# The second mixture of experts of a two-block network: rooms of 192, 96 and 32 tokens, cut into chunks of 128, 64 and 32

## The chip, the cores and the metric

The kernel runs on one core of one Trainium2 chip. The metric is the device time of one execution in microseconds; where several executions were timed, the median stands. The core has five engines with a queue of instructions each: TensorE (PE; its weight loads are listed apart, as PEld), VectorE (DVE), ScalarE (ACT), GpSimd (POOL) and SyncE (SP), which issues nearly all of the transfers from the chip's memory.

## The reference

The program is a network of two blocks on 256 tokens of width 1024. The first block has a convolution, an attention with forgetting, and a mixture of 32 experts, four for each token. The second has two layers: a hybrid mixer with a dense feed-forward part, and a hybrid mixer with a mixture of eight experts, two for each token. The change touches that last mixture alone:

```python
def moe_swiglu(x, router_w, router_b, w1, w3, w2):     # x: 256 tokens x 1024
    logits = (x @ router_w) + router_b                 # 8 experts
    top_vals, top_idx = lax.top_k(logits, 2)
    top_w = jax.nn.softmax(top_vals, axis=-1)
    gate = jnp.sum(jax.nn.one_hot(top_idx, 8) * top_w[..., None], axis=-2)
    out = jnp.zeros_like(x)
    for e in range(8):                                 # w1, w3: 1024 x 1408, w2: 1408 x 1024
        out = out + gate[..., e:e + 1] * ((silu(x @ w1[e]) * (x @ w3[e])) @ w2[e])
    return out
```

All is float32. Only the tokens that chose an expert have a gate above zero, so an expert may be computed on these tokens alone. With the inputs of the reference the eight experts are chosen by 57, 123, 49, 9, 8, 49, 165 and 52 tokens (worked out from the reference).

## The kernel before

The second mixture is the function `moe2`, the last stage of the program. Its experts are taken in eight places, p0 to p7. Place p0 is always expert 0, so that its weights can be loaded before the routing is known; the others are filled by rank, rank 1 being the expert with the most tokens. `RANK2` gives the rank that a place takes, and `ROOM2` how many tokens the place has room for:

```python
ROOM2 = [128, 256, 64, 64, 128, 128, 128, 64]
RANK2 = [0, 1, 7, 6, 2, 3, 4, 5]
```

Tokens over a place's room would go to a loop at the end (L1816 and on), whose number of turns is read at run time; one turn computes a chunk of up to 128 tokens.

The weights of an expert come in 17 loads: 11 of 1 MB, one for each slice of 128 of the hidden width 1408 (`w13`, 1024 x 256: w1 and w3 side by side), five of 1 MB with two such slices of w2 each, and one of 0.5 MB with the last. All go through SP's queue into a ring of eight tiles; a load waits until the tile that it overwrites has been read by all who read it. Each generator below yields after a load and its work, and `run` steps through it, so that two experts can be put into one order by turns.

There are three forms of an expert:

- `expert_all` (room 256, p1) takes all tokens, without gathering. `split` (L322 to L328) first makes two float32r halves of each weight tile, a cast on ACT (L325) and a difference on DVE (L328) for each 128x1024, and `mm3` (L304 to L307) multiplies by three products of the halves. 
- `expert_128` (p0, p4, p5, p6) has split weights too. Its tokens are gathered: `gather2` multiplies the transposed tokens by a matrix of zeros and ones (L1598) for a group of places at once. The tokens stand as the stationary operand and the weights stream, 256 columns at a time. `finish` applies silu and the product, and transposes the result (L1718 is the same step in the next form), and `spread` (L1650 to L1665) splits the outcome into halves `my0h` and `my0l` (for 128 also `my1h` and `my1l`), multiplies it by the matrix that puts tokens back (L1662), and adds it into `xres` with the gate.
- `expert_64` (p2, p3, p7) uses the weights unsplit as float32. Its 64 tokens take half of TensorE's columns, so two loads are worked side by side (L1732), one slice in columns 0 to 63 and one in 64 to 127; in the w2 part (L1748) the two halves of the output stand side by side.

The order of the work is written out by hand. After p0, p1 runs with p2 and p3 by turns: one load of p1, then two of p2 (later p3). Then come p4, p5, p6 and p7, one after another. Gathers stand at the half of p0 (for p2, p3, p7), of p1 (for p4, p5) and of p5 (for p6):

```python
every, few = expert(1), [expert(2), expert(3)]
while run(every, 1, lambda: gather_group((4, 5))):
    for _ in range(2):
        while few and not run(few[0], 1):
            few.pop(0)
...
run(expert(4))
run(expert(5), 99, lambda: gather_group((6,)))
run(expert(6))
run(expert(7))
```

## Time and profile before

| | us |
|---|---|
| median of 3 runs (lowest, highest) | 2324.02 (2322.54, 2326.08) |
| the profiled execution | 2327.09 |
| its span, from the first instruction to the last | 2325.3 |
| second mixture, from the first row of its gathering to the end | 1853 to 2325 |
| p0; p1 with p2 and p3; p4; p5 with a gather; p6; p7 | 58.5; 171.7; 51.5; 55.2; 50.8; 37.3 |

The stages in the last row follow one another and end at 2308.3 us; the last layer norm and the output take the rest. A profile's row of busy time says how long an engine had an instruction under way. A row of a timeline is a run of like instructions: its start, its length from the first start to the last end, engine, line, operation, the names written and read, the shape and the count. Lengths of single matmul rows overlap, since one is let in before the last has ended; what a matmul costs is read from the starts of two, or from a long run of them.

### The profile page before, as it was taken

How to read it: one execution, taken by the hardware profiler on the slowest of the kernel's cores; microseconds unless marked ns; L12 is line 12 of the kernel's file. 1: busy time of each engine (PE TensorE's matmuls, PEld its weight loads, DVE VectorE, ACT ScalarE, POOL GpSimd, SP SyncE). 2: the span in 40 equal slices, each digit the busy share in tenths (PEclk: the TensorE clock that was granted, in tenths of full speed). 3: DMA queues.
4: the chain of work that ended last, by engine and by line, in shares of the span. 5: the costliest groups of instructions: out<-in, count | busy, mean ns of one | idle time of the engine just before them, and what ended most of it. 6: DMA issues, size and time to landing. Idle time of an engine off the chain costs nothing. (4 is left out here: it accounts for less than half of the span.)

```text
span 2325.3 us, 34078 instructions
## 1 busy us (share of the span) xinstructions
PE 2158.1 (93%) x13530; PEld 1424.9 (61%) x13530; DVE 1126.3 (48%) x2048; ACT 785.4 (34%) x1313; POOL 34.9 (2%) x45
## 2 busy tenths in 40 slices
PE   6999999899999889998797999999999899999996
PEld 4888533333333333333235988998888788777983
DVE  3976222323322322322236657654665775337883
ACT  3354211101111111111104655444465564335771
POOL 0000000000000000000000010000001000000000
PEclk9999899998999989999897999999999989999998
DMA  9757689998999999999898334555533467779884
GB/s 395 282 217 271 242 321 417 416 407 344 410 416 416 416 416 412 415 415 416 367 416 335 134 109 164 182 189 183 188 130 110 166 223 275 281 298 349 330 329 197
DMA packets 122630, 697.52 MB, mean 300 GB/s; under 512 B 11120, under 2 KB 11648, under 8 KB 63936
## 3 DMA queue, kind: packets, MB, share of 16 engines
q1 hardware_dynamic: 121120, 690.54, 76.1%
q0 software_dynamic: 1344, 4.73, 0.7%
q8 instruction: 109, 1.79, 0.3%
q14 instruction: 57, 0.47, 0.1%
HBM read 694.18 MB, written 1.05 MB: 299 GB/s over the span
## 5 line engine op out<-in xcount | busy, mean ns | idle before, releaser
L328 DVE TENSOR_TENSOR wl<-w,wh 128x1024 fp32r<-128x1024 f32 (+1 forms) x393 | 476.9, 1223 | 256.7 <-ACT wh L325 247.5
L325 ACT CAST wh<-w 128x1024 fp32r<-128x1024 f32 (+1 forms) x393 | 407.4, 1044 | 304.5 <-PE acc L306 65.7
L962 PE MATMUL h<-w,xg 128*64 128x512 f32 x1280 | 302.0, 620 | 0.0
L997 PE MATMUL s<-w,hm 128*64 128x512 f32 (+1 forms) x1088 | 252.1, 651 | 17.6 <-DVE hm L985 14.1
L962 PEld LDWEIGHTS h<-w,xg 128*64 128x64 f32 x1280 | 93.7, 142 | 186.7 <-issue 182.2
L306 PE MATMUL acc<-xTl,wh 128*128 128x256 f32 x528 | 149.7, 284 | 0.0
L305 PE MATMUL acc<-xTh,wh 128*128 128x256 f32 x528 | 149.7, 283 | 0.0
L307 PE MATMUL acc<-xTh,wl 128*128 128x256 f32 x528 | 149.6, 283 | 0.0
L973 ACT COPY hs<-h 128x512 f32<-128x512 f32 x34 | 19.9, 585 | 373.2 <-PE h L962 290.5
L997 PEld LDWEIGHTS s<-w,hm 128*64 128x64 f32 (+1 forms) x1088 | 62.2, 132 | 130.8 <-issue 95.0
L956 PE MATMUL h<-w,xg 128*32 128x512 f32 x896 | 114.4, 635 | 17.6 <-DMA w<-in_wei 17.6
L973 DVE COPY hs<-h 128x512 f32<-128x512 f32 x20 | 13.8, 691 | 235.9 <-PE h L962 235.9
L910 PEld LDWEIGHTS t<-oh,xh 128*128 128x128 f32 x512 | 70.5, 209 | 76.2 <-ACT xg L911 32.2
L911 ACT ACTIVATE xg<-t,modc,a 128x128 f32<-128x128 f32 (+3 forms) x128 | 55.4, 440 | 182.2 <-PE t L910 126.4
L307 PEld LDWEIGHTS acc<-xTh,wl 128*128 128x128 f32 x528 | 99.3, 188 | 4.2 <-issue 3.1
L305 PEld LDWEIGHTS acc<-xTh,wh 128*128 128x128 f32 x528 | 99.3, 188 | 2.5 <-issue 1.5
L306 PEld LDWEIGHTS acc<-xTl,wh 128*128 128x128 f32 x528 | 99.3, 188 | 2.0 <-issue 1.1
L306 PE MATMUL f<-fxl,wh 128*128 128x256 f32 x352 | 99.9, 284 | 0.0
L305 PE MATMUL f<-fxh,wh 128*128 128x256 f32 x352 | 98.9, 282 | 0.7 <-ACT fxh L1236 0.7
L307 PE MATMUL f<-fxh,wl 128*128 128x256 f32 x352 | 99.3, 283 | 0.0
L910 PE MATMUL t<-oh,xh 128*128 128x128 f32 (+3 forms) x512 | 85.5, 309 | 14.2 <-ACT xg L911 7.1
L1011 ACT CAST ysh<-ys 128x512 fp32r<-128x512 f32 x34 | 21.0, 618 | 222.6 <-DVE ys L1010 207.4
(540 smaller groups left out, 4294.8 us busy)
## 6 DMA issues: line engine op xcount, KB each, us to landing
w<-in_wei SPq DMA_DIRECT2D x256, 1024.0 KB, 18.4
w<-in_weo SPq DMA_DIRECT2D x128, 1024.0 KB, 19.9
w<-in_wm SPq DMA_DIRECT2D x128, 1024.0 KB, 5.8
w<-in_wf SPq DMA_DIRECT2D x33, 1024.0 KB, 4.8
w<-in_w2in SPq DMA_DIRECT2D x32, 1024.0 KB, 5.1
w<-in_wada SPq DMA_DIRECT2D x24, 1024.0 KB, 9.7
w<-in_win SPq DMA_DIRECT2D x16, 1024.0 KB, 8.6
w<-in_w2out SPq DMA_DIRECT2D x8, 1024.0 KB, 4.9
```

The lines of the kernel that those rows point to most:

```text
L305: T.matmul(o, l[0], r[0], start=start, stop=False)
L306: T.matmul(o, l[0], r[1], start=False, stop=False)
L307: return T.matmul(o, l[1], r[0], start=False, stop=stop)
L325: A.copy(wh[:, :m], w[:, o:o + m])
L328: V.tensor_sub(wl[:, :m], w[:, o:o + m], wh[:, :m])
L910: T.matmul(pt[:, 0:n], xh2[:, tt, k * P:(k + 1) * P], oh[:, tt, 0:n], start=tt == 0, stop=tt == 1)
L911: taken.append(A.activation(xg[:, k, 0:n], pt[:, 0:n], AF.Identity, bias=sh2[:, k:k + 1], scale=a2[:, k:k + 1]))
L956: T.matmul(ph[0][0][32 * q:32 * q + 32, :].rearrange("p (i c) -> p i c", i=4), chunks[0][:, k], w5[:, q % 2, q // 2], start=k == 0, stop=k ...
L962: T.matmul(p[j][64 * gu:64 * gu + 64, :], xs[:, k], w[:, gu * D + j * 512:gu * D + j * 512 + 512], start=k == 0, stop=k == 7)
L973: (A.copy if j == 0 else V.tensor_copy)(hs[:, j], p[j])
L997: T.matmul(p[r, :], hm[:, kk * 2 + k], w[:, k * D + hf * 512:k * D + hf * 512 + 512], start=kk == 0 and (small or k == 0), stop=kk == 3 an ...
L1011: A.copy(yp[0], ys)
```

## The change

The rooms become 128, 192, 32, 32, 128, 64, 96 and 96 for p0 to p7, each cut into chunks of 128, 64 or 32 (`CHK2`), and the ranks are dealt anew: p2 and p3 take ranks 6 and 7, p5 rank 5, p6 and p7 ranks 3 and 4. With the counts above every expert fits its room. One generator, `expert2`, replaces the three forms: each load of weights is used for all chunks of a place. Chunks of 128 work as before with split weights; those of 64 as before with the unsplit weights of two loads; a chunk of 32 is new: it takes a quarter of TensorE's columns, so that w1 and w3 of two loads stand side by side (L1704), and in the w2 part two slices and two halves of the output (L1731). Only places with a chunk of 128 split their weights. In p1 the tiles of two loads are read twice, by the chunk of 128 as they come and by that of 64 when both are there.

p2 and p3 run by turns with p1 as before, and p5 now by turns with p4. The gathers after p0 stand at the half of p0 (p1, p2, p3), p1 (p4, p5) and p4 (p6, p7). The transposed tokens `xT` move to the buffer that the gather's operand `xtp` also uses. The loads and their order on SP's queue stay: 136 for the eight experts.

```diff
--- before.py
+++ after.py
@@ -37,8 +37,11 @@
-ROOM2 = [128, 256, 64, 64, 128, 128, 128, 64]
-RANK2 = [0, 1, 7, 6, 2, 3, 4, 5]
+CHK2 = [[(0, 128)], [(0, 128), (128, 64)], [(0, 32)], [(0, 32)], [(0, 128)], [(0, 64)], [(0, 64), (64, 32)], [(0, 64), (64, 32)]]
+ROOM2 = [sum(n for _, n in c) for c in CHK2]
+RANK2 = [0, 1, 6, 7, 2, 5, 3, 4]
...
-                xT = pair([P, 8, S], "mx", 1)
+                xT = pair([P, 8, S], "xt", 1)
...
-                        xs.append(wk.tile([P, 8, 64], F32, tag="mx64", name=nm("mx64"), bufs=3) if room == 64
-                                  else tuple(t[:, :, o:o + 128] for t in big))
+                    for _, (_, room), _ in items:
+                        xs.append(big if room == 128
+                                  else wk.tile([P, 8, room], F32, tag=f"mx{room}", name=nm(f"mx{room}"), bufs=3))
...
-                def expert_all(w13, w2, gate):
...
-                def expert_128(w13, w2, xg, item):
...
-                def expert_64(w13, w2, xg, item):
...
+                def expert2(w13, w2, xs, items):
+                    rooms = [room for _, (_, room), _ in items()]
+                    hid = [hidden_pair() if n == 128 else wk.tile([P, FT2, n], F32, tag=f"mhm{n}", name=nm("mhm"), bufs=1 if n == 64 else 2) for n in rooms]
+                    def finish(n, hp, f0, nf, ph):
+                        if n == 128:
...
+                            return
+                        r = slice(0, 64 * nf)
+                        s = wk.tile([P, P], F32, tag="mss", name=nm("mss"), bufs=3)
+                        if n == 64:
+                            A.activation(s[r], ph[r, 0:P], AF.Silu)
+                            V.tensor_tensor(s[r], s[r], ph[r, P:S], op=ALU.mult)
+                        else:
+                            A.copy(s[r], ph[r, 0:P])
                         pt = bank()
+                        T.transpose(pt[:, r], s[r], ident[r, r])
+                        if n == 64:
+                            A.copy(hp[:, f0:f0 + nf], pt[:, r].rearrange("p (f s) -> p f s", s=64))
+                        else:
+                            p4 = pt[:, r].rearrange("p (f g s) -> p f g s", g=2, s=32)
+                            s = wk.tile([P, 2, 32], F32, tag="msg", name=nm("msg"), bufs=2)
+                            A.activation(s[:, 0:nf], p4[:, :, 0], AF.Silu)
+                            V.tensor_tensor(hp[:, f0:f0 + nf], s[:, 0:nf], p4[:, :, 1], op=ALU.mult)
                     pend = []
+                    def finish_all():
+                        while pend:
+                            finish(*pend.pop(0))
                     for f0 in range(0, FT2, 2):
                         nf = min(2, FT2 - f0)
+                        phs = [bank("b", 6) for _ in rooms]
                         ws = []
                         for fi in range(nf):
                             ws.append(load(w13(f0 + fi)))
+                            if rooms[0] == 128:
+                                w = split(ws[fi], 256)
+                                for k in range(8):
+                                    mm3(phs[0][:, fi * S:(fi + 1) * S], tuple(x[:, k] for x in xs[0]), cview(w, k, 256, 0, 256), k == 0, k == 7)
                             if fi < nf - 1:
                                 yield "step"
+                        for n, x, ph in zip(rooms, xs, phs):
+                            if n == 128:
+                                continue
+                            for k in range(8):
+                                for fi, w in enumerate(ws):
+                                    if n == 64:
+                                        T.matmul(ph[64 * fi:64 * fi + 64, 0:S], x[:, k], w[:, k * S:(k + 1) * S], start=k == 0, stop=k == 7)
+                                    else:
+                                        for gu in range(2):
+                                            c = 64 * fi + 32 * gu
+                                            T.matmul(ph[c:c + 32, 0:P], x[:, k], w[:, k * S + gu * P:k * S + gu * P + P],
+                                                     start=k == 0, stop=k == 7)
+                        finish_all()
+                        pend += [(n, hp, f0, nf, ph) for n, hp, ph in zip(rooms, hid, phs)]
                         yield "step"
                     yield "half"
+                    gts = [back(item) for item in items()]
+                    pys = [[bank("b", 6) for _ in range(2 if n == 128 else 1)] for n in rooms]
                     for f0 in range(0, FT2, 2):
                         nf = min(2, FT2 - f0)
                         w = load(w2(f0, nf), nf * D)
+                        if rooms[0] == 128:
+                            wp = split(w, D, nf * D)
+                        if rooms[0] < 128:
+                            finish_all()
+                        for n, hp, py in zip(rooms, hid, pys):
+                            for fi in range(nf):
+                                f = f0 + fi
+                                for hf in range(2):
+                                    c = fi * D + hf * 512
+                                    if n == 128:
+                                        mm3(py[hf], sl(hp, slice(None), f), cview(wp, fi, D, hf * 512, hf * 512 + 512), f == 0, f == FT2 - 1)
+                                    elif n == 64:
+                                        T.matmul(py[0][64 * hf:64 * hf + 64, :], hp[:, f], w[:, c:c + 512], start=f == 0, stop=f == FT2 - 1)
+                                    else:
+                                        r = 64 * hf + 32 * fi
+                                        T.matmul(py[0][r:r + 32, :], hp[:, f], w[:, c:c + 512], start=f0 == 0, stop=f >= FT2 - 2)
+                            finish_all()
                         yield "step"
+                    for n, py, gt in zip(rooms, pys, gts):
+                        spread(py, *gt, [(0, slice(0, P)), (1, slice(0, P))] if n == 128 else [(0, slice(0, 64)), (0, slice(64, P))])
...
+                def items(p):
+                    return [(columns(route2.posm, p), c, columns(route2.gp, p)) for c in CHK2[p]]
...
-                    gather_group((2, 3, 7))
-                run(expert(0), 99, half0)
-                every, few = expert(1), [expert(2), expert(3)]
-                while run(every, 1, lambda: gather_group((4, 5))):
+                    gather_group((1, 2, 3))
...
+                most, few = expert(1), [expert(2), expert(3)]
+                while run(most, 1, lambda: gather_group((4, 5))):
                     for _ in range(2):
                         while few and not run(few[0], 1):
                             few.pop(0)
                 while few:
                     run(few.pop(0))
-                run(expert(4))
-                run(expert(5), 99, lambda: gather_group((6,)))
+                most, few = expert(4), expert(5)
+                while run(most, 1, lambda: gather_group((6, 7))):
+                    run(few, 1)
+                run(few)
                 run(expert(6))
                 run(expert(7))
```

The next rows are TensorE's order while p1 and p2 run by turns, before: p1's product of three with all tokens as the streamed operand (`mxh`, `mxl`), then two of p2's loads at 64 wide.

```order
L305 MATMUL b_15128<-mxh_14221,wh_15124 128x256
L306 MATMUL b_15128<-mxl_14222,wh_15124 128x256
L307 MATMUL b_15128<-mxh_14221,wl_15125 128x256
L1732 MATMUL b_15185<-w_15186,mx_2494_14860 64x256
L1732 MATMUL b_15185<-w_15188,mx_2494_14860 64x256
```

After, in the same place: the chunk of 128 of p1 has its second load (`wh_15216`), and then the chunk of 64 of p1 reads the two tiles that were held for it (`w_15138`, `w_15210`).

```order
L308 MATMUL b_15136<-wh_15216,mxh_14855 128x256
L309 MATMUL b_15136<-wl_15217,mxh_14855 128x256
L310 MATMUL b_15136<-wh_15216,mxl_14856 128x256
L1700 MATMUL b_15137<-w_15138,mx_2496_14863 64x256
L1700 MATMUL b_15137<-w_15210,mx_2496_14863 64x256
```

Behind these 16 products of the chunk of 64 come 32 of p2's chunk of 32 (L1704). What was one block with all tokens and one 64 wide is now one of 128, one of 64 and one of 32.

The second place is TensorE's order where an unsplit expert goes from its last slice of w1 and w3 into w2. Before, in p7 (64):

```order
L1718 MATMUL t_18516<-cz,ms_18513 128x128
L1732 MATMUL b_18519<-w_18520,mx_2496_14862 64x256 x8
L1718 MATMUL t_18533<-cz,ms_18530 128x128
L1613 MATMUL t_18536<-cz,posm_14847 128x128 x2
L1748 MATMUL b_18541<-w_18542,mhm_18389 64x512
L1718 MATMUL t_18547<-cz,ms_18544 128x64
L1748 MATMUL b_18541<-w_18542,mhm_18389 64x512 x3
L1748 MATMUL b_18541<-w_18554,mhm_18389 64x512 x4
L833 MATMUL t_18602<-cnt_14317,perm_14316 8x1
L1748 MATMUL b_18541<-w_18560,mhm_18389 64x512 x4
```

After, in p6 (64 and 32):

```order
L1700 MATMUL b_17813<-w_17815,mx_2908_17178 64x256 x8
L1704 MATMUL b_17814<-w_17815,mx_2909_17179 32x128 x16
L1667 MATMUL t_17844<-cz,mss_17841 128x128
L1667 MATMUL t_17849<-cz,mss_17847 128x128
L1727 MATMUL b_17864<-w_17866,mhm_17489 64x512
L1619 MATMUL t_17854<-cz,posm_14847 128x128 x2
L1619 MATMUL t_17859<-cz,posm_14847 128x128 x2
L1727 MATMUL b_17864<-w_17866,mhm_17489 64x512 x2
L1667 MATMUL t_17871<-cz,mss_17868 128x64
L1667 MATMUL t_17876<-cz,mss_17874 128x64
L1727 MATMUL b_17864<-w_17866,mhm_17489 64x512
L1731 MATMUL b_17865<-w_17866,mhm_17490 32x512 x4
```

The transpositions, the two broadcasts of the positions and the blocks of each load stand twice in it, once for each chunk.

The third place is the end of the last expert. Before, its one `spread` follows the last load of w2:

```order
L1748 MATMUL b_18541<-w_18578,mhm_18389 64x512 x2
L1662 MATMUL b_18586<-my0h_18582,mgt_18539 128x512
L1662 MATMUL b_18587<-my0h_18582,mgt_18539 128x512
L1662 MATMUL b_18594<-my0h_18582,mgt_18539 128x512
L1662 MATMUL b_18595<-my0h_18582,mgt_18539 128x512
L1662 MATMUL b_18586<-my0l_18583,mgt_18539 128x512
L1662 MATMUL b_18587<-my0l_18583,mgt_18539 128x512
```

After, two follow one another, the second reading the next `my0h`:

```order
L1727 MATMUL b_18359<-w_18424,mhm_17984 64x512 x2
L1731 MATMUL b_18360<-w_18424,mhm_17985 32x512 x2
L1635 MATMUL b_18434<-my0h_18430,mgt_18352 128x512
L1635 MATMUL b_18435<-my0h_18430,mgt_18352 128x512
L1635 MATMUL b_18442<-my0h_18430,mgt_18352 128x512
L1635 MATMUL b_18434<-my0l_18431,mgt_18352 128x512
L1635 MATMUL b_18435<-my0l_18431,mgt_18352 128x512
L1635 MATMUL b_18443<-my0h_18430,mgt_18352 128x512
L1635 MATMUL b_18442<-my0l_18431,mgt_18352 128x512
L1635 MATMUL b_18443<-my0l_18431,mgt_18352 128x512
L840 MATMUL t_18470<-cnt_14317,perm_14316 8x1
L1635 MATMUL b_18454<-my0h_18450,mgt_18357 128x512
```

## Rows read from the trace of the kernel before

**Rows 1.** The page: span, and busy time by engine.

```profile
span 2325.3 us, 34078 instructions
PE 2158.1 (93%) x13530; PEld 1424.9 (61%) x13530; DVE 1126.3 (48%) x2048; ACT 785.4 (34%) x1313; POOL 34.9 (2%) x45
```

**Rows 2.** Windows of the stages p1 to p7: length, busy times, clock, DMA share, GB/s.

```profile
1941.80:2113.50 171.70, 170.10 (x1168) 126.67 (x1166) 67.54 (x115) 52.68 (x108) 0.00 (x0) 1.00 0.77 298
2113.50:2165.00 51.50, 51.28 (x357) 47.01 (x356) 47.27 (x52) 38.58 (x47) 0.00 (x0) 1.00 0.93 350
2165.00:2220.20 55.20, 54.98 (x386) 50.17 (x385) 49.32 (x62) 40.37 (x55) 0.00 (x0) 1.00 0.87 319
2220.20:2271.00 50.80, 50.60 (x352) 46.31 (x350) 44.45 (x51) 34.71 (x43) 0.00 (x0) 1.00 0.89 337
2271.00:2308.30 37.30, 36.52 (x245) 18.79 (x244) 5.61 (x17) 3.55 (x13) 0.00 (x0) 1.00 0.60 245
```

**Rows 3.** Windows of single steps, TensorE: length, busy time, clock, DMA.

```profile
1956.83:1960.44 3.61, 3.61 (x34) 1.00 1.03 399
1960.52:1966.38 5.86, 5.86 (x49) 1.00 0.92 347
2017.77:2021.36 3.59, 3.59 (x18) 1.00 0.67 230
2063.45:2069.23 5.78, 5.78 (x25) 1.00 0.83 294
```

**Rows 4.** Timeline of TensorE in p7.

```profile
2278.08 0.33 PE L1718 MATMUL t<-cz,ms 128*128 128x128 f32 x1
2278.34 3.67 PE L1732 MATMUL b<-w,mx 128*64 128x256 f32 x32
...
2293.70 0.61 PE L1613 MATMUL t<-cz,posm 128*128 128x128 f32 x4
```

**Rows 5.** Timelines of TensorE in the first block and a mixer.

```profile
527.68 1.07 PE L956 MATMUL h<-w,xg 128*32 128x512 f32 x8
...
190.36 0.67 PE L646 MATMUL tr<-modc,wr 128*32 128x1 f32 x16
190.96 0.39 PE L305 MATMUL acc<-athi,wh 128*128 128x256 f32 x1
...
1403.78 1.97 PE L1447 MATMUL t<-cz,nrst 128*64 128x128 f32 x32
```

**Rows 6.** Groups by line, second mixture: busy, mean ns, idle before.

```profile
L328 DVE TENSOR_TENSOR wl<-w,wh 128x1024 fp32r<-128x1024 f32 x165 | 202.3, 1237 | 96.1 <-ACT wh L325 88.2 <-PE b L307 6.1 <-PE b L1748 0.2
L325 ACT CAST wh<-w 128x1024 fp32r<-128x1024 f32 x165 | 172.4, 1049 | 120.8 <-PE b L307 56.9 <-PE b L306 36.3 <-DMA w<-in_wm 14.7
```

**Rows 7.** Waits of TensorE's weight loads, p1 to p6: total, times, longest.

```profile
PEld b L1662 <- ACT my0h L1656: 5.0, 5, 1.7
```

**Rows 8.** Timeline of all engines, end of p7.

```profile
2306.16 0.58 ACT L1656 CAST my0h<-b 128x512 fp32r<-128x512 f32 x1 [10.40 <-PE b L1748]
...
2306.80 0.73 PE L1662 MATMUL b<-my0h,mgt 64*128 64x512 f32 x4 [0.74 <-ACTq L1817]
...
2308.07 2.73 DVE L1665 SCALAR_TENSOR_TENSOR xres<-b,gp,xres 128x512 f32<-128x512 f32 x4 [0.60 <-PE b L1662]
```

**Rows 9.** Timelines of ACT, POOL and TensorE, start of the mixture.

```profile
1860.89 1.05 ACT L1568 CAST xth<-xres 128x1024 fp32r<-128x1024 f32 x1 [2.30 <-DVE xres L1182]
...
1862.30 2.37 POOL L1569 TENSOR_TENSOR xtl<-xres,xth 128x1024 fp32r<-128x1024 f32 x1
...
1868.55 0.28 PE L307 MATMUL t<-mxh,wr 128*32 128x256 f32 x1
...
1876.16 0.63 PE L1598 MATMUL t<-mohr,xtl 128*128 128x256 f32 x2
```

**Rows 10.** Window of the first block's experts: busy times, clock, DMA share, GB/s.

```profile
650.00:700.00 50.00, 46.02 (x246) 18.03 (x248) 14.59 (x32) 6.41 (x14) 0.00 (x0) 0.93 1.01 416
```

**Rows 11.** DMA issues, 1887 to 2308 us: count, KB each, us to landing.

```profile
w<-in_wm SPq DMA_DIRECT2D x118, 1024.0 KB, 6.1
```

More of the change, by code (lines that the diff above doesn't have):

```diff
@@ L746, in topk, with slot_col @@
         yield
+    def slot_col(chunk):
+        i = SLOTS.index(chunk)
+        return KA["slot"][:, i:i + 1]
     class Routing:
@@ L1586, in gather2 @@
                         if room == 128 and big is None:
[L1587 removed]
+                            big = pair([P, 8, P], "mx", 1)
                     if n < S:
@@ L1599, in gather2 @@
                                          start=q + tt == 0, stop=q + tt == 2)
-                        for (_, room, _), o, x in zip(items, where, xs):
-                            if room == 64:
-                                A.copy(x[:, k], pt[:, o:o + 64])
+                        for (_, (_, room), _), o, x in zip(items, where, xs):
+                            if room < 128:
+                                A.copy(x[:, k], pt[:, o:o + room])
                             else:
@@ L1608, in back @@
                 def back(item):
-                    pos, room, gate = item
+                    pos, chunk, gate = item
                     pt = bank()
@@ L1682, in expert_128 @@
                     pend = []
+                    def finish_all():
+                        while pend:
+                            finish(*pend.pop(0))
                     for f0 in range(0, FT2, 2):
                         nf = min(2, FT2 - f0)
-                        ph = bank("b", 6)
-                        for fi in range(nf):
-                            w = split(load(w13(f0 + fi)), 256)
-                            for k in range(8):
-                                mm3(ph[:, fi * S:(fi + 1) * S], tuple(x[:, k] for x in xg), cview(w, k, 256, 0, 256), k == 0, k == 7)
-                            yield "step"
@@ L1789, in run @@
                     return True
-                ready[0], = gather2([([pos0[:, tt:tt + 1] for tt in range(2)], 128, None)], hidden_pair())
+                ready[0] = gather2([([pos0[:, tt:tt + 1] for tt in range(2)], (0, 128), None)])
                 def half0():
@@ L1819, in moe2 @@
                         w13, w2 = weights(nc.sync.value_load(ei[0:1, 0:1], min_val=0, max_val=NE2 - 1))
-                        more = [pe[:, 0:1], pe[:, 1:2]], CAP2, [ge[:, 0:1], ge[:, 1:2]]
-                        for _ in expert_128(w13, w2, gather2([more])[0], lambda: more):
+                        more = [pe[:, 0:1], pe[:, 1:2]], (0, CAP2), [ge[:, 0:1], ge[:, 1:2]]
+                        for _ in expert2(w13, w2, gather2([more]), lambda: [more]):
                             pass
```

133 lines of the change are left out of this document (26 added, 107 removed).

## The prediction

> **What bounds the kernel now.** I read the page's first lines first: TensorE is busy for 2158.1 of 2325.3 us, and no other engine for half of it [rows 1]. The change lies in the second mixture, so I cut that into its stages with the view of windows. From p1 to p6 TensorE is busy at least 99% of each stage (170.10 of 171.70, 51.28 of 51.50, 54.98 of 55.20, 50.60 of 50.80) at a granted clock of 1.00, the upper of its two levels, 2.4 GHz. The transfers take 0.77 to 0.93 of their engines there, 0.60 in p7 [rows 2]. So TensorE sets the end of these stages, with the transfers not far behind. The price of a part is then TensorE's time for it, and I must ask at the end whether the transfers can keep up with a faster TensorE.
>
> Next I took the time of single steps from windows around them. With all 256 tokens one load of w1 and w3 takes 5.86 us and one of w2 5.78. With 64 tokens two loads of w1 and w3, side by side, take 3.61, and two of w2 3.59, so 1.80 for one [rows 3]. Between the end of the first of these windows and the start of the second, where the width changes from 64 to full, lie 0.08 us.
>
> **Prices of the forms.** A chunk of 128 has a stage of its own: p6, 50.8 us with its `spread` [rows 2]. The room of 256 has 11 x 5.86 + 5.5 x 5.78 = 96.3 (the w2 part is 5.5 loads). The room of 64 has six pairs by 3.61 and 5.5 by 1.80; six transpositions at 0.26 each (2278.08 to 2278.34, both changes of width in it); the broadcasts of the positions at 0.5 to 0.6 [rows 4]; and the `spread` at 1.4 (two rows of 0.73 [rows 8]): 21.7 + 9.9 + 1.6 + 0.5 + 1.4 = 35.
>
> The chunk of 32 has no row of its own kind. For a pair of loads it has 32 products, each of which would stand as two rows, like the 32 rows for 16 products of the 64 form: 64 rows of 128 columns, four quarters of the array at once. If the four truly run side by side, each group of four takes half of what a group of two with 256 columns takes: 3.61 / 16 / 2 = 0.113, and a pair 16 x 0.113 = 1.8 us. From the other side: sixteen rows 32 wide and one column long start within 190.36 to 190.96, so 0.0375 each; four of them are 0.15, and the pair 2.4. Eight rows of 512 columns, 32 wide, take 1.07, or 0.134 each, so quarters do run together there [rows 5]. I take 0.13 for a group of four, midway, hence 2.1 for a pair and 5.8 pairs (the last has one load, and its rows fill only half): about 12.3. The w2 part has half the time of the 64 form, since two slices and two halves run at once: 5.5 x 0.9 = 5.0, and I take 5.4 for the blocks that are short. With transpositions 1.6, broadcasts 0.5 and `spread` 1.4 the chunk of 32 comes to 21.3; bounds from those rows are 19.5 and 23.
>
> **The sum.** Before, p1 to p7 take 171.7 + 51.5 + 55.2 + 50.8 + 37.3 = 366.5 [rows 2]. By forms: p1 to p3 96.3 + 2 x 35 = 166.3, so 5.4 is left over, 4.4 of it a gather (p5, which has one, is 55.2 - 50.8 = 4.4 longer than p6).
> - p1 to p3 after: 50.8 + 35 + 2 x 21.3 + 5.4 = 133.8, where 171.7 stood: -37.9.
> - p4 and p5 by turns: 51.5 + 35 + 4.4 = 90.9.
> - p6 and p7: 35 + 21.3 = 56.3 each.
> - the end of p7, 37.3 - 35 = 2.3, as before.
>
> Together 339.6: 26.9 less. Gathers stay three after p0, so they cancel, but for their members.
>
> Against that stand four charges. (1) `spread` has one buffer for `my0`, and where two follow one another, in p1, p5 and p6, or p3 behind p2, the second waits for cast and difference. The five waits on `my0h` now come to 5.0 us [rows 7], so 1.0 each; I add four: +4. (2) At the end of p7 a `spread` is bare: from the cast at 2306.16 to the last sum at 2308.07 + 2.73 it is some 4.6 us, and after the change two stand there. The second overlaps the first's sums, so I add about 3 [rows 8]: +3 (0 to 4.6). (3) At the start `xth` and `xtl` must wait until the router, the last reader of `xT`, is done at 1868.55 + 0.28. The two casts and differences that began earlier take 1.05 on ACT, then 2.37 on POOL each; the second difference ends near 1868.83 + 1.05 + 2 x 2.4 = 1874.7, the cast hidden under the first, or some 1.5 later with what queues before it on POOL, and its first reader runs at 1876.16 [rows 9]: +1 (0 to 3). (4) The order of p1 to p7 has 198 changes of width on TensorE where it had 58. Some 70 of the 140 more are in the prices above, with their transpositions. For the other 70 one row has 0.08 a change, which is 5.6, and another bounds it by half of 0.26 (two changes with a transposition between them), which is 9.1 [rows 3, 4]. Since small blocks follow wide ones here that are already in flight, I take 4 (0 to 9).
>
> So -26.9 + 12 = -15. The profiled execution had 2327.1, which makes 2312; the median of the three runs lies 3.1 below it, so **2309**.
>
> The Trainium skill says in "TensorEngine Tiling (Array Packing)", section "Key Properties", that a change of the tiling mode, and not only of the tile, drains TensorE. By it no change is hidden under the block before and the upper end holds, 9 instead of 4 and 2314 in all; the 0.08 us between two windows here agrees that a change is seen, and its small size speaks for the lower figure.
>
> **What costs nothing.** Five places split their weights before, three after: 2 x 33 = 66 pairs of 1.05 on ACT and 1.24 on DVE go, 151 us of work [rows 6]. But these ran beside a TensorE that was busy 99% of the stage, so their going earns nothing. The new copies and products of the chunk of 32 stand on the same two engines, which have more room than before.
>
> **The transfers.** The loads are the same 136 in the same order. At the best rate seen, 416 GB/s [rows 10], a load of 1024 KB [rows 11] takes 2.52 us, an expert of 16.5 such loads 41.6. p1 to p3 need 124.8 and TensorE 133.8; p4 and p5 83.2 against 90.9; p6 and p7 41.6 against 56.3. TensorE stays the later one everywhere, by 7% at the narrowest. Within p1 the w13 part has one load of p1 and two of p2 in a turn: two turns need six loads, 15.1 us, and TensorE has 2 x 2.9 for the chunk of 128, 3.6 for that of 64, and 2 x 2.1 with transpositions, 14.4. There the transfers are late by 0.7 a pair, unless the ring of eight tiles has stock. I charge nothing for it, and keep up to 10.
>
> **The rivals.**
> *The small products are bound by their number.* This one ends on the other side. Thirty-two rows of 128 columns, 64 wide, take 1.97, so 0.0616 each [rows 5]. If that is the price of a row however narrow, a pair of the 32 form has 64 x 0.0616 = 3.94 instead of 2.1; there are 4 x 5.5 = 22 full pairs, and, with 1.84 more each, 40 us. The time is then about 2349. For it: these are the only rows of 128 columns in a narrow form. Against it: at 64 wide only two go side by side, and half of a row of 256 columns, 3.61 / 32 / 2 = 0.056, would by itself bound them; and the rows at 0.0375 show a quicker start. It decides, that is, the gain is gone, at 15 / 22 = 0.7 more a pair: 2.8 a pair, or 0.043 a row. The Trainium skill gives in "TensorE: Matmul & The Clock Gate", section "Wait — 56ns, not 53.3ns?", floors of about 25 ns from start to start, and 62 ns per matmul where the hardware's decoding is off; by the latter an estimate of a pair is 3.97, by the former 1.6, and the rows at 0.0375 in this trace speak for the former. Chance 0.13.
>
> *The transfers take over.* Loads are held longer (p1's tiles until the chunk of 64 has read them), and a ring of eight with two held has less stock. If p1's w13 part and the w2 part of p2 (three loads, 7.6 us, against 6.6) wait as worked out, and p4 with p5 loses some, 8 to 10 us go: 2318. For it: 0.93 of the DMA was used already in p4 [rows 2]. Chance 0.13.
>
> *Everything hides.* Quarters at 0.113, no wait at the `spread`s and no cost at the changes of width: 26.9 - 2 (end and start), and 4 x 1.7 less for the quarters, make 2292. Chance 0.08.
>
> *The rooms don't hold.* If the device's routing differs from the reference's counts, one turn of the last loop costs a chunk of 128, at least 50.8: 2360. The counts fit with 5 places to spare at p4 (123 in 128), and more in every other place. Chance 0.02.
>
> The forecast itself, 2301 to 2317, has 0.64.
>
> **How the numbers follow.** What a measurement of this kernel can tell from no change is about 0.2%, 4.6 us: 2319.4 to 2328.6. Faster: the forecast, the case where all hides, and half of the transfers' case, 0.64 + 0.08 + 0.07 = 0.79. Same: the rest of that case and a mild form of the first rival, 0.07. Slower: the first rival and the last, 0.14. The range 2293 to 2326 holds the forecast, nearly all of the case that hides, and that of the transfers, and leaves the side of the many small products out.
>
> **What would show it.** In the changed trace the blocks of the 32 form (L1704) should take 1.8 to 2.4 us a pair; near 3.9 the first rival is right. p1 to p3 should last about 134 us and TensorE stay above 97% busy; gaps before L308 or L1700 that end with a load are the transfers. The weight loads of `spread` should wait on `my0h` nine times where they waited five. p6 and p7 at 56 each test the whole price; if they show 70 and more, the forecast is wrong in its main term. A turn in the loop behind p7 would show as matmuls after the last `spread`.

## The result: slower by 1%

The changed kernel takes 2346.74 us, the median of four runs (2340.44 to 2350.22); the kernel before takes 2323.28 beside it. The ratio is 1.0099, with a 95% interval of 1.008 to 1.0119. The forecast was 2309, and 2293 to 2326 as its range. The execution that was profiled took 2350.22.

The page of the changed kernel answers to [rows 1]. TensorE is busy for about as long as before, though much of its work was taken away:

```profile
span 2348.5 us, 35670 instructions
PE 2164.2 (92%) x14411; PEld 1372.4 (58%) x14411; DVE 1052.8 (45%) x1986; ACT 719.6 (31%) x1297; POOL 34.6 (1%) x45
```

The windows of the stages answer to [rows 2], with the same columns. They are p1 with p2 and p3, p4 with p5, p6, and p7 with its end:

```profile
1941.10:2094.40 153.30, 147.20 (x1449) 95.93 (x1447) 63.07 (x103) 49.82 (x102) 0.00 (x0) 1.00 0.85 334
2094.40:2212.00 117.60, 109.12 (x625) 77.86 (x625) 52.09 (x64) 41.02 (x88) 0.00 (x0) 0.91 0.77 294
2212.00:2270.60 58.60, 57.73 (x652) 30.89 (x652) 10.68 (x25) 6.14 (x26) 0.00 (x0) 1.00 0.81 308
2270.60:2331.00 60.40, 59.05 (x661) 31.74 (x661) 12.23 (x29) 6.14 (x26) 0.00 (x0) 0.99 0.42 156
```

Their sum is 389.9 where p1 to p7 took 366.5 before: 23.4 more, which is the whole difference of the two profiled executions (2350.2 - 2327.1 = 23.1). Against the forms of the forecast the stages stand so:

| stage | before | forecast by forms | after | after - forecast |
|---|---|---|---|---|
| p1, p2, p3 | 171.7 | 133.8 | 153.3 | +19.5 |
| p4, p5 | (p4 51.5; a 64: 37.3) | 90.9 | 117.6 | +26.7 |
| p6 | | 56.3 | 58.6 | +2.3 |
| p7 and its end | | 58.6 | 60.4 | +1.8 |

Less the 12 us of charges that the forecast added, 38 are missed, as the profiled 2350 against 2312 says. Two stages hold nearly all of it: in p4 with p5 the clock is 0.91 and TensorE idles 8.5 us; in p1 to p3 it idles 6.1.

The small products, the first rival, are not the reason, though its 2349 lies near the result. This is TensorE's timeline in p6, a chunk of 64 (L1700) and one of 32 (L1704) by turns; the columns are those of [rows 4]:

```profile
2222.32 1.96 PE L1704 MATMUL b<-w,mx 128*32 128x128 f32 x64
2224.20 0.44 PE L1667 MATMUL t<-cz,mss 128*128 128x128 f32 x2
2224.57 3.67 PE L1700 MATMUL b<-w,mx 128*64 128x256 f32 x32
2228.17 1.95 PE L1704 MATMUL b<-w,mx 128*32 128x128 f32 x64
2230.06 0.44 PE L1667 MATMUL t<-cz,mss 128*128 128x128 f32 x2
```

From start to start a pair of the chunk of 32 takes 2224.20 - 2222.32 = 1.88 us, 0.029 for each of its 64 rows. The forecast had 2.1, the rival 3.94.

What happens in p4 with p5 is seen in one turn. First ACT's timeline, then TensorE's, of the changed kernel; in brackets the idle time ahead of a row and what ended it:

```profile
2120.20 0.38 ACT L1656 CAST mhh<-t 128x256 fp32r<-128x256 f32 x1 [0.26 <-PE t L1654]
2123.80 0.27 ACT L1669 COPY mhm<-t 128x128 f32<-128x128 f32 x1 [3.22 <-PE t L1667]
2123.96 1.99 ACT L328 CAST wh<-w 128x1024 fp32r<-128x1024 f32 x2
```

```profile
2122.86 0.65 PE L1700 MATMUL b<-w,mx 128*64 128x256 f32 x2
2123.43 0.33 PE L1667 MATMUL t<-cz,mss 128*128 128x128 f32 x1
...
2125.06 0.38 PE L308 MATMUL b<-wh,mxh 128*128 128x256 f32 x1 [1.30 <-ACT wh L328]
2126.32 0.58 PE L309 MATMUL b<-wl,mxh 128*128 128x256 f32 x1 [0.88 <-DVE wl L331]
2126.70 0.41 PE L310 MATMUL b<-wh,mxl 128*128 128x256 f32 x1
2126.91 0.41 PE L308 MATMUL b<-wh,mxh 128*128 128x256 f32 x1
2127.12 0.41 PE L309 MATMUL b<-wl,mxh 128*128 128x256 f32 x1
```

ACT has nothing to do for 3.22 us, because its next instruction is the copy of p5's transposed values (L1669), and the transposition (L1667) stands on TensorE behind a whole block of p4. The cast of p4's next tile comes behind that copy, so TensorE waits for the cast, and once more for the difference. Then its products start every 0.21 us instead of 0.12. The windows of a piece ahead of the wait and of the piece behind it show why (length, busy times, clock, DMA):

```profile
2121.00:2124.00 3.00, 2.76 (x20) 2.05 (x18) 0.23 (x2) 0.20 (x2) 0.00 (x0) 1.00 0.94 396
2126.30:2131.50 5.20, 5.18 (x23) 4.98 (x23) 1.10 (x1) 0.00 (x0) 0.00 (x0) 0.50 0.93 359
```

The granted clock went from 1.00 to 0.50, from the upper level, 2.4 GHz, to the lower, 1.2. From the first product of such a block to what follows it, four turns took 4.20, 6.47, 5.70 and 6.47 us where 2.95 is the undisturbed length. The first of them kept its clock; its wait for the cast was 0.57 us, that of the others 1.30. But the longer wait alone does not decide: in e4 below, which leaves p4 and p5 as they are, a block behind waits of 1.30 and 0.87 us takes 4.20 at the full clock:

```profile
2150.90:2155.10 4.20, 3.32 (x24) 3.00 (x24) 2.35 (x2) 0.91 (x1) 0.00 (x0) 1.00 1.01 352
```

Over the whole of p4 with p5 TensorE waits four times for a cast and four times for a difference, 8.0 us of the 8.5 that it idles (total, times, longest):

```profile
PE b L308 <- ACT wh L328: 4.5, 4, 1.3
PE b L309 <- DVE wl L331: 3.5, 4, 0.9
```

### The profile page after: what moved, and what is told of

Same layout as the page of the kernel before. It is cut to its first block, busy times and chain, and to the rows that moved or that the text cites. A ratio compares the mean times of both kernels' runs of the same rounds, so it can differ in the third digit from the quotient of the medians.

```text
span 2348.5 us, 35670 instructions
## 1 busy us (share of the span) xinstructions
PE 2164.2 (92%) x14411; PEld 1372.4 (58%) x14411; DVE 1052.8 (45%) x1986; ACT 719.6 (31%) x1297; POOL 34.6 (1%) x45
## 3 DMA queue, kind: packets, MB, share of 16 engines
HBM read 694.18 MB, written 1.05 MB: 296 GB/s over the span
## 5 line engine op out<-in xcount | busy, mean ns | idle before, releaser
L331 DVE TENSOR_TENSOR wl<-w,wh 128x1024 fp32r<-128x1024 f32 (+1 forms) x327 | 392.8, 1216 | 204.4 <-ACT wh L328 202.4
L328 ACT CAST wh<-w 128x1024 fp32r<-128x1024 f32 (+1 forms) x327 | 336.4, 1044 | 221.7 <-PE acc L309 73.9
L308 PE MATMUL acc<-xTh,wh 128*128 128x256 f32 x528 | 149.7, 284 | 0.0
L309 PE MATMUL acc<-xTl,wh 128*128 128x256 f32 x528 | 149.7, 284 | 0.0
L1004 PEld LDWEIGHTS s<-w,hm 128*64 128x64 f32 (+1 forms) x1088 | 61.9, 131 | 131.4 <-issue 94.2
L308 PEld LDWEIGHTS acc<-xTh,wh 128*128 128x128 f32 x528 | 99.3, 188 | 2.5 <-issue 1.5
L309 PEld LDWEIGHTS acc<-xTl,wh 128*128 128x128 f32 x528 | 99.3, 188 | 2.0 <-issue 1.1
L308 PE MATMUL f<-fxh,wh 128*128 128x256 f32 x352 | 99.3, 283 | 0.7 <-ACT fxh L1242 0.7
L309 PE MATMUL f<-fxl,wh 128*128 128x256 f32 x352 | 99.3, 283 | 0.0
L1700 PE MATMUL b<-w,mx 128*64 128x256 f32 x704 | 96.6, 386 | 0.3 <-DVE xres L1638 0.3
```

What stands on the lines that cost most here:

```text
L308: T.matmul(o, l[0], r[0], start=start, stop=False)
L309: T.matmul(o, l[0], r[1], start=False, stop=False)
L328: A.copy(wh[:, :m], w[:, o:o + m])
L331: V.tensor_sub(wl[:, :m], w[:, o:o + m], wh[:, :m])
L1004: T.matmul(p[r, :], hm[:, kk * 2 + k], w[:, k * D + hf * 512:k * D + hf * 512 + 512], start=kk == 0 and (small or k == 0), stop=kk == 3 an ...
L1700: T.matmul(ph[64 * fi:64 * fi + 64, 0:S], x[:, k], w[:, k * S:(k + 1) * S], start=k == 0, stop=k == 7)
```

## The experiments

Theory A is the order on ACT with the clock behind it. The rivals are late transfers (B), the changes of width (C), and in e8 a late landing of p4's own tiles (D). The edits are against the changed kernel, but for e14.

**e1: p4, then p5.**

```diff
-                most, few = expert(4), expert(5)
-                while run(most, 1, lambda: gather_group((6, 7))):
-                    run(few, 1)
-                run(few)
+                run(expert(4), 99, lambda: gather_group((6, 7)))
+                run(expert(5))
```

> p4 and p5 run one after the other instead of by turns; nothing else changes. In the changed kernel p4 with p5 took 117.6 us (2094.4 to 2212.0), 26.7 more than the 90.9 of the forecast, and TensorE's granted clock stood at 0.54 to 0.70 in three stretches of it. Theory A (the cast of p4's next weight tile stands on ACT behind p5's copy L1669, which waits for a transposition at the end of TensorE's block; the wait then lowers the clock): without turns p4 takes about 51 and p5 with the gather 39 to 44, 92 to 96 in all, so the time falls by 21 to 26, to 2321 to 2326, and the clock of the stretch is 1.00. Theory B (the transfers are late, since a pair of p5 holds two tiles of the ring of eight): p5 alone is then bound by its loads, 41.6 to 44, p4 by its own 50.8, so 97 to 100 and a time near 2328 to 2330. Theory C (the changes of width between chunks cost the time): they fall from some 24 to 8 in these places, under 2 us, and the time stays above 2340.

Measured 2330.67, ratio to before 1.0030 (1.0020 to 1.0041). The windows of p4 and p5:

```profile
2089.70:2148.40 58.70, 58.23 (x389) 52.28 (x389) 47.96 (x54) 38.52 (x75) 0.00 (x0) 0.97 0.85 311
2148.40:2185.30 36.90, 35.49 (x239) 18.36 (x238) 4.69 (x12) 3.66 (x13) 0.00 (x0) 1.00 0.88 351
```

Together 95.6 instead of 117.6, as theory A has it. C is out, and p5 at 36.9 is not bound by its loads as B has it, though the total, 2330.67, missed A's 2321 to 2326 and lies nearer to B's. The clock of p4 is below 1.00 in its first 4 us alone (0.57), behind p3's `spread`. The total gained 16, not 22: the profiled execution of the changed kernel was the slowest of its four, and p6 went from 58.6 to 61.9 and p7 from 60.4 to 61.4. In p6 blocks are now cut that were whole before, as its timeline shows (whole blocks stand in the fence of p6 above):

```profile
2198.49 0.65 PE L1700 MATMUL b<-w,mx 128*64 128x256 f32 x2
2199.07 0.41 PE L1704 MATMUL b<-w,mx 128*32 128x128 f32 x4
2199.41 0.44 PE L1667 MATMUL t<-cz,mss 128*128 128x128 f32 x2
2199.78 3.67 PE L1700 MATMUL b<-w,mx 128*64 128x256 f32 x30
2203.38 1.94 PE L1704 MATMUL b<-w,mx 128*32 128x128 f32 x60
```

The 30 rows that are left take 3.60, as long as the whole 32; the two that were put ahead cost 0.58 on top, and the four 0.34.

**e2: load and split one step ahead.**

```diff
+                                if f + 1 < FT2:
+                                    ahead.append(first(f + 1))   # first: load(w13(f)) and split
```

> Every expert with a chunk of 128 loads and splits its next slice of w1 and w3 before it gives the turn away, so that the cast on ACT is issued ahead of the other expert's finish; all else, the turns too, stays. Theory A (casts stuck behind the copy L1669 of the unsplit chunk): p4 with p5 falls from 117.6 to 92 to 98 us and its clock rises to 1.00, p1 to p3 fall by 2 to 6 from 153.3, the time comes to 2318 to 2326. Theory B (late transfers): the loads only move by one place in the queue, and both stretches stay within 3 us of what they were, 2343 to 2348. If only part of the waits goes, the rest must be seen as waits of L308 or L309 on wh or wl.

Measured 2336.39 (1.0063, 1.0038 to 1.0087). p4 with p5:

```profile
2086.60:2195.90 109.30, 102.95 (x624) 72.03 (x623) 52.08 (x64) 41.02 (x88) 0.00 (x0) 0.98 0.81 314
```

It fell by 8.3, less than theory A expected and more than B; p1 to p3 fell to 149.1, as expected, and the total missed A's 2318 to 2326. TensorE still idles 6.4, of which 5.5 are waits for casts and differences, three of each: a later cast now stands behind the copy. The clock rose from 0.91 to 0.98, but the length of this stage and its clock differ also where an edit leaves the stage alone (the table behind e14), so the 8.3 are not a measure of the order.

**e3: the 32 uses my1 in spread.**

```diff
-                        ys[i] = pair([P, 512], f"my{i}", 1)
+                        ys[i] = pair([P, 512], f"my{first + i}", 1)   # first = 1 for a chunk of 32
```

> The chunk of 32 puts its halves for spread into my1, which only the chunk of 128 uses otherwise, so that a spread of 32 behind one of 64 (p6, p7) need not wait for my0. In the changed kernel the second spread of p6 begins at 2268.7 and its four rows on my0h take 1.92 where 0.7 are enough; at the end of p7 it is 2.51. If the single buffer is what makes the second spread wait, p6 falls by 1 to 1.5, the end of p7 by 1.5 to 2, and p3's spread behind p2's is as before: 2342 to 2344. If it is the sums into xres (DVE, four of 0.7 for each spread) that set the pace, under 0.7 in all.

Measured 2337.34 (1.005, 1.0034 to 1.0067). p6, and p7 with its end:

```profile
2203.00:2260.80 57.80, 57.47 (x654) 30.89 (x654) 10.17 (x25) 6.13 (x26) 0.00 (x0) 1.00 0.80 303
2260.80:2319.10 58.30, 57.95 (x658) 31.09 (x657) 11.87 (x27) 6.13 (x26) 0.00 (x0) 1.00 0.46 173
```

The windows are 0.8 and 2.1 shorter, but the second ends with TensorE's last row of `spread`, and the sums into `xres` go on behind it. These are the last sums of this run, then those of the changed kernel:

```profile
2316.99 5.35 DVE L1638 SCALAR_TENSOR_TENSOR xres<-b,gp,xres 128x512 f32<-128x512 f32 x8
2330.35 2.73 DVE L1638 SCALAR_TENSOR_TENSOR xres<-b,gp,xres 128x512 f32<-128x512 f32 x4 [0.18 <-PE b L1635]
```

From p7's start to the last sum it is 61.5 us instead of 62.5, and from p6's first product to the end of the span 135.5 instead of 136.5. So the second buffer earns about 1 us in both places together, less than the 2.5 to 3.5 expected: mostly the sums set the pace. The rest of the fall in the total is not due to it: p4 with p5, which the edit leaves alone, took 109.9 in this execution, with a clock of 0.95.

**e4: 128 for p6 and p7.**

```diff
-... [(0, 64), (64, 32)], [(0, 64), (64, 32)]]
+... [(0, 128)], [(0, 128)]]
```

> p6 and p7 get a room of 128 as one chunk with split weights, instead of 96 as chunks of 64 and 32; nothing else changes. By the rows, 64 and 32 take 58.6 us in p6 and 60.4 in p7 with its end, one chunk of 128 took 50.8 in p6 before, so the two places fall by 119.0 - (50.8 + 52.5) = 15 to 16 and the time to 2330 to 2332. The rival, that casts would now come late in p6 and p7 too because nothing but the turn's partner matters: then the fall is under 8, 2339 or more, and L308 waits on wh there.

Measured 2333.05 (1.0038, 1.0026 to 1.0051): 13.7 less. p7 with its end came to 52.9 instead of 60.4, p6 only to 56.6 from its first product (2204.2 to 2260.8), behind p5. So 64 and 32 together are dearer than one chunk of 128, by 7.5 and 2; the forecast of 15 to 16 for the two places was too high. Of the rest some lies in p4 with p5, which the edit leaves alone: 114.7 to that product in this execution, with the same 4.5 and 3.5 us of waits as in the changed kernel, but a clock of 0.94.

**e8: the copy L1669 on VectorE.**

```diff
-                            A.copy(hp[:, f0:f0 + nf], pt[:, r].rearrange("p (f s) -> p f s", s=64))
+                            V.tensor_copy(hp[:, f0:f0 + nf], pt[:, r].rearrange("p (f s) -> p f s", s=64))
```

> The copy of the transposed hidden values of a chunk of 64 (L1669) is made by VectorE instead of ScalarE; nothing else. In the turns of p4 and p5 of the changed kernel the cast of p4's next tile stands on ACT right behind this copy, and TensorE then waits 1.3 us for the cast and 0.9 for the difference. Theory A (order on ACT): the cast is now early and only the difference, which stands behind the copy on DVE, is late: TensorE waits 1.2 to 1.5 a turn instead of 2.2, some turns keep the full clock, p4 with p5 falls from 117.6 to 105 to 114. Theory D (the wait comes from the late landing of p4's tiles, not from the order): the casts begin when they began, p4 with p5 stays within 2 us.

Measured 2339.2 (1.0067, 1.005 to 1.0084). p4 with p5:

```profile
2094.65:2203.00 108.35, 102.21 (x626) 71.56 (x627) 53.52 (x70) 39.42 (x82) 0.00 (x0) 0.98 0.82 313
```

TensorE's waits for cast and difference in it:

```profile
PE b L309 <- DVE wl L331: 5.1, 4, 1.4
PE b L308 <- ACT wh L328: 0.6, 1, 0.6
```

The waits for the cast are gone but for one, and the difference is late at each turn, by up to 1.4: theory A, to the size of the wait. D is out, since the loads, their order and the turns are those of the changed kernel, and one copy was moved to another queue. The stage is 9 shorter, but only 2.3 of that are waits; the rest goes with the clock (0.98 instead of 0.91), and this stage was found as short as 104.3 where an edit leaves it alone (e7), so the 9 are not all shown to come from the copy.

**e10: turns of two loads.**

```diff
-                while run(most, 1, lambda: gather_group((6, 7))):
-                    run(few, 1)
+                while run(most, 2, lambda: gather_group((6, 7))):
+                    run(few, 2)
```

> p4 and p5 take turns of two loads each instead of one, so that a block of 48 products of p4 is followed by a whole pair of p5; nothing else. The transposition of p5 still stands at or before the end of p4's block, but the pair of p5 (3.6 us) comes behind it and covers the cast and the difference (1.05 and 1.22 us). Theory A: p4 with p5 falls from 117.6 to 91 to 97, the clock of the stretch is 1.00, the time falls by 21 to 26 to 2320 to 2326. If transfers or the widths were the cause, interleaving in itself keeps it above 105.

Measured 2330.74 (1.0034, 1.0018 to 1.005). p4 with p5, and ACT in one of its turns:

```profile
2089.30:2190.40 101.10, 99.54 (x623) 71.11 (x623) 52.28 (x64) 40.88 (x88) 0.00 (x0) 0.98 0.87 333
```

```profile
2120.22 0.37 ACT L1656 CAST mhh<-t 128x256 fp32r<-128x256 f32 x1 [0.98 <-PE t L1654]
2120.49 1.99 ACT L328 CAST wh<-w 128x1024 fp32r<-128x1024 f32 x2
2123.81 0.28 ACT L1662 ACTIVATE mss<-b 128x128 f32<-128x128 f32 x1 [1.33 <-PE b L1700]
2123.99 1.99 ACT L328 CAST wh<-w 128x1024 fp32r<-128x1024 f32 x2
2127.11 0.27 ACT L1669 COPY mhm<-t 128x128 f32<-128x128 f32 x1 [1.14 <-PE t L1667]
```

The casts of both loads now stand ahead of the copy, TensorE has no wait for a cast or a difference left in the stage, and 16.5 of the 26.7 are gone with the turns still there. Behind the first 4 us the clock is whole:

```profile
2093.30:2190.40 97.10, 95.56 (x607) 68.00 (x606) 48.58 (x60) 40.88 (x88) 0.00 (x0) 1.00 0.88 337
```

The stage stays 4 above the expected 97, and the time 5 above 2320 to 2326; its blocks are cut too.

**e7: 64 for p2 and p3.**

```diff
-CHK2 = [..., [(0, 32)], [(0, 32)], ...]
+CHK2 = [..., [(0, 64)], [(0, 64)], ...]
```

> p2 and p3 get a room of 64 each instead of 32 (and are gathered in a group of their own, about 4 us more on TensorE in p0); p1 and the turns stay. TensorE's own work in p1 to p3 grows by 2 x (35 - 21) = 28 and the loads stay. If p1 to p3 (153.3 us, where the forms add up to 134) are bound by the transfers in the w1 and w3 part, where loads land every 2.5 us and casts start as their tile lands, most of the growth hides in that time: 155 to 165. If TensorE's order and its many small blocks are the bound, the growth is seen in full: 175 to 182, and the time is 2370 to 2378.

Measured 2355.66 (1.0135, 1.0118 to 1.0153). p1 to p3:

```profile
1946.50:2114.70 168.20, 166.83 (x1097) 105.46 (x1095) 66.82 (x105) 50.45 (x102) 0.00 (x0) 0.99 0.81 310
```

That lies between the two expectations: 15 more, where the prices of the forms add 28. TensorE was busy for 19.6 more (166.83 instead of 147.20), and its idle time fell from 6.1 to 1.4. The loads are the same, so they alone do not bind the stage; the 8.4 of added work that TensorE's busy time does not show were most likely small blocks in the changed kernel's 153, which was not tested apart. p4 with p5, which the edit leaves alone, took only 104.3 here; most of p5's blocks are whole on TensorE in this run, and only one pair of waits for cast and difference is left.

**e5: 64 for p6 and p7, with e1.**

```diff
-... [(0, 64), (64, 32)], [(0, 64), (64, 32)]]
+... [(0, 64)], [(0, 64)]]
```

> p6 and p7 get a room of 64 (their experts have 52 and 49 tokens), and p4 and p5 run one after the other as in e1. In e1, p6 and p7 took 61.9 and 61.4 with the end and p5, with 64 tokens, 36.9. If TensorE bounds a chunk of 64 that follows another, p6 and p7 take 37 and 38, 48 less than in e1: 2282. If the loads bound it, 41.6 each at 416 GB/s, with some stock left from p4: 40 less, 2290 to 2293, and the DMA share in p6 and p7 is 0.97 or more.

Measured 2290.7 (0.9851, 0.9834 to 0.9869). p6, and p7 with its end:

```profile
2191.50:2230.40 38.90, 35.81 (x241) 19.06 (x239) 5.69 (x13) 3.79 (x13) 0.00 (x0) 1.00 1.02 417
2230.40:2272.40 42.00, 37.23 (x246) 18.67 (x244) 6.43 (x18) 3.79 (x13) 0.00 (x0) 1.00 0.84 343
```

Together 80.9 instead of 123.3 in e1, 42 less: the case in which the loads bind. In p6 the transfers are at their best rate, 417 GB/s; in p7, where the loads run out, the mean share is 0.84.

**e13: e1 and e4 together.** The diffs are those of e1 and e4:

```diff
+                run(expert(4), 99, lambda: gather_group((6, 7)))
+                run(expert(5))
...
+... [(0, 128)], [(0, 128)]]
```

> Both costly parts of the change are undone together: p4 and p5 run one after the other (e1), and p6 and p7 have one chunk of 128 each (e4). What is left of the change is p1 with 128 and 64 and p2 and p3 with 32. If the costs simply add, the time is 2330.7 (e1) less the 123.3 that p6 and p7 took there, plus 50.8 + 52.5: 2311 to 2313, which is 0.5% under the kernel before. If the turns of p4 and p5 only pushed work that then falls due in p6 and p7, it stays above 2318.

Measured 2318.4 (0.9982, 0.9973 to 0.9992). With both parts undone the change is faster by 0.2%. It is 6 above the sum and just above the 2318 that was named for the rival, since p6 does not come to 50.8 behind an unsplit expert: 56.8, with 0.98 of the transfers used. This is not work pushed from the turns, which are gone here. At p6's start the first difference stands on DVE behind the four sums of p5's `spread`, TensorE waits 3.4 us for it, and the clock is then 0.62 for 4.5 us; what the transfers add was not separated.

```profile
2185.40:2242.20 56.80, 53.20 (x357) 49.03 (x356) 48.74 (x54) 38.75 (x50) 0.00 (x0) 0.97 0.98 378
```

**e12: e5 with turns of two and four in p1 to p3.**

```diff
-                while run(most, 1, lambda: gather_group((4, 5))):
-                    for _ in range(2):
+                while run(most, 2, lambda: gather_group((4, 5))):
+                    for _ in range(4):
```

> e5 (p6 and p7 with 64, p4 then p5) with longer turns in p1 to p3: two loads of p1, then four of p2 or p3, instead of one and two. The loads' mix and TensorE's work stay, the blocks become longer. In e5 p1 to p3 took 153.0 where the forms add to 134. If the short blocks and the order around them cost the 19, p1 to p3 fall by 8 or more, to 145 or less, and the time to 2283 or less. If the transfers bound the w1 and w3 part (33 loads of 2.5 us are 83 us there), they stay at 150 to 155 and the time at 2288 to 2293.

Measured 2281.21 (0.982, 0.9802 to 0.9838). p1 to p3:

```profile
1936.60:2082.40 145.80, 142.23 (x1448) 95.82 (x1446) 60.98 (x98) 48.63 (x102) 0.00 (x0) 1.00 0.85 339
```

7 less than the 153.0 of e5, just short of the 8 expected, while this stage took 153.0 to 153.3 in the four runs that leave it alone (the changed kernel, e1, e4, e5). So the short blocks and the order around them were a good third of the 19; the rest is not resolved further.

**e11: p1 with p2, p4 with p3.** It is e5 with other partners and turns of two loads:

```diff
+                most, few = expert(1), expert(2)
+                while run(most, 2, lambda: gather_group((4, 5))):
+                    run(few, 2)
...
+                most, few = expert(4), expert(3)
+                while run(most, 2, lambda: gather_group((6, 7))):
+                    run(few, 2)
+                run(few)
+                run(expert(5))
```

> A version meant to beat both kernels: p1 by turns of two loads with p2, then p4 by turns of two loads with p3, then p5, p6 and p7 with 64 each, one after another. Each stage mixes an expert that TensorE bounds with one that the loads bound. By the forms: p1 with p2 86 + 21 + gather 4 = 111 (loads 83), p4 with p3 51 + 21 + 4 = 76, but its loads 83, p5 to p7 three times 37 to 41.6, loads 125, so 83 + 120 to 125 behind 111 to 116: 316 to 322 in all, where e5 took 330.4: the time is 2276 to 2283. If the transfers bind from the start (291 for p1 to p7 at the best rate), it cannot go under 2250; if the turns bring back waits for casts, it is no better than e5, 2290.

Measured 2282.26 (0.9824, 0.981 to 0.9837), within the expected span, and not better than e12.

**e14: the kernel before with 64 for p5 and p6.**

```diff
-ROOM2 = [128, 256, 64, 64, 128, 128, 128, 64]
+ROOM2 = [128, 256, 64, 64, 128, 64, 64, 64]
```

> The kernel before with one line changed: p5 and p6 (52 and 49 tokens) get a room of 64 instead of 128; no chunk of 32, no new turns. Before, p5 without its gather and p6 took 50.8 each, p7 with 64 took 37.3. If TensorE's price of the form decides, p5 to p7 are three times 37, or 41.6 where the loads bind: 18 to 27 less, 2296 to 2305. That would tell that the gain of e5 and e12 comes from giving an expert the cheapest single form that holds it. If unsplit experts in a row starve on loads more than that, it is within 10 of the kernel before, 2313 or more.

Measured 2297.0 (0.9884, 0.9865 to 0.9902): one line of the old kernel gives more than half of the best gain. These rooms are tighter: 52 and 49 tokens stand in 64, and an expert with more would cost a turn of the last loop.

**p4 with p5 over all runs.** From p4's first product to p6's, with TensorE's waits for the cast (L308) and for the difference (L309) in it:

| run | edit to p4 and p5 | waits: cast, difference (us) | clock | length (us) |
|---|---|---|---|---|
| changed kernel | | 4.5, 3.5 | 0.91 | 117.6 |
| e4 | none | 4.5, 3.5 | 0.94 | 114.7 |
| e3 | none | 2.6, 4.9 | 0.95 | 110.0 |
| e7 | none | 1.3, 0.9 | 0.96 | 103.3 |
| e2 | split one step ahead | 2.9, 2.6 | 0.98 | 109.3 |
| e8 | copy on VectorE | 0.6, 5.1 | 0.98 | 108.2 |
| e10 | turns of two loads | none | 0.98 | 101.1 |
| e1 | no turns | 0, 0.3 | 0.98 | 95.6 |

The four runs without an edit here differ by 14 us, so e2 and e8 show by their waits what the order does, and not by their lengths. The two runs that leave at most 0.3 us of these waits are the two shortest.

## Why the prediction was wrong

- **Prices of the forms: right.** 1.88 for a pair of the 32 form (2.1 taken), 58.6 for p6 (56.3), 36.9 for 64 alone in e1 (35).
- **The sum for p4 and p5 by turns, 51.5 + 35 + 4.4 = 90.9: this step failed.** It added TensorE's times and put the wait for a split at nothing, because TensorE had been busy 99% and ACT and DVE "have more room than before". The 99% held for the old order. By turns with p5, a copy that waits for TensorE stands ahead of the cast on ACT's queue, so a split of 1.05 and 1.22 us is late. The stage took 117.6: 8.0 of the 26.7 more are waits for cast and difference. No rival named it. e8 moves one copy and shows the cast early and the difference late, as this order demands; e10 and e1, which change the blocks as well, leave at most 0.3 us of these waits and take back 16.5 and 22.
- **The clock: not considered.** At 1.00 in all stages before [rows 2], it fell behind these waits. Three blocks of 24 products took 6.47, 5.70 and 6.47 where the first, at the full clock, took 4.20: 2.3 + 1.5 + 2.3 = 6 us. The first 4 us of p4 stand at 0.57 too, in the changed kernel as in e1 and e10; by an estimate from these two figures that costs some 2 us. How many blocks the lower clock hits differs between executions; this one had the longest time of the four. Waits and clock make some 16 of the 26.7. The other 10, which e10 still has, were not separated; cut blocks are part of them.
- **p1 to p3, mis-sized:** 133.8 against 153.3. TensorE was busy for 147.2 of them, so 13 of the 19.5 lie in its own rows, and it waits only 2.8 us in all for casts there. The second rival named transfers in this stage, at up to 10 us with the ring; ACT's casts do wait for landing tiles, in three places for 7.7 us, but that is ACT's wait, and TensorE sees no more of it than its 2.8 (total, times, longest, in the changed kernel):

```profile
ACT wh L328 <- DMA w<-in_wm: 7.7, 3, 3.1
PE b L308 <- ACT wh L328: 2.8, 2, 1.5
```

  Longer blocks take back some 7 (e12). How the rest divides was not separated.
- **Changes of width, mis-sized:** 0.08 each was read from a seam between whole blocks. Where a block is cut, its first two rows cost 0.58 more (e1). The Trainium skill's sentence that a change of the tiling mode drains TensorE ("TensorEngine Tiling (Array Packing)", section "Key Properties") points the same way; the runs here do not show a drain itself.
- **`spread`: right at the end, too high between.** At the end of p7 it is 8.5 us from the first cast (2324.54) to the last sum (2333.08) where 4.6 stood before: 3.9 more, 3 forecast. The weight loads wait on `my0h` seven times for 5.3 us, not nine times, where before it was five times for 5.0; the forecast had added 4 for this. A second buffer earns 1 us (e3).
- **p6 and p7: forecast rightly and not drawn on.** By its own prices 64 and 32 were 56.3 where 128 is 50.8; only ranks 3 and 4, moved from 128 to 96, pay this, 11 us in two places by the forecast, 9.5 by e4.

## What to carry to other kernels

A busy share of 99% says that an engine was fed in the old order, not that its feeders have slack: before two streams share engines, follow the in-order queue of the feeding engine and see which instruction stands ahead of the next operand's producer, and what that waits for. Give turns the length that covers the feeder's latency (two loads here instead of one), and price each place by the cheapest single form that holds it, since two forms for one expert cost more than the next larger form.

## What the runs showed of the hardware

- Four quarters of TensorE's columns run side by side down to 0.029 us a row of 128 columns; 16 groups of four took 1.88 us.
- A block 64 wide of 32 rows takes 3.60 us; with two rows put ahead of a transposition, 0.58 + 3.60.
- The granted clock fell from 1.00 to 0.50 in three blocks of four, behind a wait of 1.30 us and then one of 0.88, in a stage whose TensorE was busy 93% of the time. In e4 it fell behind two waits of this length and not behind a third, and it stayed at 1.00 behind single waits of 1.40 (e8). What decides is not shown.
